# Row maxima over 1024 keys in one two-bank PSUM tile that a recurrence's first stage also uses

## The chip, the cores and the metric

One Trainium2 chip, one core. The metric is the device time of one execution in microseconds; the kernel before was run three times and its median is used. The profiled execution is a further one.

## The reference

Two layers of an encoder over 1024 tokens of width 1024. Each layer projects its input, runs four mixers side by side, and follows them with an output projection, a cross attention to 256 memory tokens and a mixture of experts, each with a layer norm. Two of the mixers are softmax attentions of four heads over all 1024 keys (GQA with head width 64, and MLA with 96); the other two are linear recurrences (RWKV-7 and HGRN2), in both directions. What matters here is the attention:

```
s = q . k * scale              (1024 queries x 1024 keys, per head)
p = exp(s - max over keys) / sum
o = p . v
```

## The kernel before

**The order.** Each layer's mixers are written as Python generators. `weave` advances two of them in proportion to given costs: `rwkv` (the RWKV-7 recurrence) and `beside`, which first runs the attention to its end and then HGRN2 and the preparation of the memory attention. That gives the order in which the program is written; the tile framework's scheduler then fixes one order per engine, in which instructions that are ready may pass others. On the chip each engine works through its own order and waits by semaphores.

**The attention** (lines 1398 to 1465) is cut into eight units per layer, each of two heads and 512 queries; four of GQA, then four of MLA. `row_max` computes, for a unit, the largest score of each query, with one pass of rounded operands: for each head j and each block t of 128 queries, two matmuls of 512 keys (line 1409), each into a PSUM tile of one bank, each followed by a VectorE maximum (line 1410) over its 512 columns. One more VectorE instruction joins the halves (line 1413); then, for each head, four small matmuls turn the maxima into a row (line 1417) and ScalarE copies that row, negated, into the 65th or 97th row of an operand (line 1418), so that the later score matmuls subtract the maximum. `attend` then takes the 1024 keys in eight steps of 128: score matmuls into tile `b` (line 1441), an exponential on ScalarE (line 1443), value matmuls into `o` (line 1429), and an addition on GpSimd that collects the denominators (line 1432). `attention` runs the `row_max` of one unit and the `attend` of the unit before it in lockstep, one step of each in turn, `attend` first; the row maxima of the first unit stand alone.

**The recurrence** runs up to four of its units at a time in lockstep, each in another stage. A unit's first stage uses PSUM tile `a0`: two gate matmuls (lines 961 and 966) that ScalarE reads through a tanh, and twice 32 small matmul records (line 1027) into two banks, each bank read by a masked VectorE product (line 1029). The later stages use `a1`.

**PSUM before**, eight banks of 512 floats per partition: `a0` two tiles of one bank, `a1` two, `b` two, `c` one (row maxima alone, and for the first unit `c`, `b`, `b` in turn), `o` one.

**Key buffers.** The rounded keys `kh0`, `kh1` and their remainders have one buffer per name. An MLA unit with new keys (the fifth and the seventh) therefore can't load them before the scores of the unit in front are done.

Of the kernel before, what the change touches and what calls it, by code (L numbers as in the profile page):

```python
# [13 lines left out]
S = 1024  # L14
# [168 lines left out]
F32R = mybir.dt.float32r  # L183
I32 = mybir.dt.int32
U32 = mybir.dt.uint32
AF = mybir.ActivationFunctionType
ALU = mybir.AluOpType
AX = mybir.AxisListType
PSUM = bass.MemoryType.PSUM
# [123 lines left out]
def ahead(gen):  # L313

    return chain([next(gen)], gen)
# [439 lines left out]
def lockstep(gens, group=0):  # L755

    gens = list(gens)
    while gens:
        n = 0
        for g in list(gens):  # L760
            try:
                c = next(g) or SMALL
            except StopIteration:
                gens.remove(g)
                continue
            n += c
            if not group:
                yield c
        if group:
            yield n  # L770
# [121 lines left out]
def rwkv_unit(k, e):  # L892

    nc, A, V, S, T, G = k.nc, k.A, k.V, k.S, k.T, k.G
    hp, d, hf, first, pl, lo, kn, kds, zr, zk, kept = (e[n] for n in (
        "hp", "d", "hf", "first", "pl", "lo", "kn", "kds", "zr", "zk", "kept"))
    hw, wa, seg, mask, blk4, lvl, id64 = (e[n] for n in ("hw", "wa", "seg", "mask", "blk4", "lvl", "id64"))
    w = 0

    def bank():  # L900
        return k.t(e["ps"], [128, 512], f"a{w}")

    def tl(shape, tag, bufs=1):
        return k.t(pl, shape, tag, bufs=bufs)
# [4 lines left out]
    q = lambda p: slice(64 * p, 64 * p + 64)  # L909

    def pairs(fn, cols, evac, byhead=False):


        if byhead:

            b = [bank() for _ in range(2)]
            for i in range(4):
                for h in range(2):
                    for p in range(2):
                        fn(b[h][:, cols * i:cols * i + cols], i, h, p)  # L920
            for h in range(2):
                evac(b[h][:, :4 * cols].rearrange("q (m c) -> q m c", c=cols), slice(h, 8, 2))
        elif cols == 128:
            for g in range(2):
                b = bank()
                for m in range(4):
                    i, h = divmod(4 * g + m, 2)
                    for p in range(2):
                        fn(b[:, cols * m:cols * m + cols], i, h, p)
                evac(b[:, :4 * cols].rearrange("q (m c) -> q m c", c=cols), slice(4 * g, 4 * g + 4))  # L930
        else:
            b = bank()
            for m in range(8):
                i, h = divmod(m, 2)
                for p in range(2):
                    fn(b[:, cols * m:cols * m + cols], i, h, p)
            evac(b.rearrange("q (m c) -> q m c", c=cols), slice(0, 8))
# [17 lines left out]
    j = 2 * d + hp  # L955
# [4 lines left out]
    b = bank()  # L960
# [4 lines left out]
    b = bank()  # L965
# [47 lines left out]
    if e["n"] == 3:  # L1013
# [3 lines left out]
        b = bank()  # L1017
# [8 lines left out]
    for x, dst in ((0, AB), (1, AK)):  # L1026
        pairs(lambda o, i, h, p: T.matmul(o[q(p)], BK[q(h), x, 2 * i + p], AR[q(h), :, 2 * i + p],
                                          start=True, stop=True),
# [7 lines left out]
    for pb in range(8):  # L1036
        b = pb % 4
# [12 lines left out]
    for n in range(1, 8):  # L1050
        s, r = (7 - n, slice(8 - n, 8)) if d == 0 else (n, slice(0, n))
# [6 lines left out]
    i, o = (lo_, hi_) if d == 0 else (hi_, lo_)  # L1058
# [19 lines left out]
    w = 1  # L1078
# [9 lines left out]
    def tok(src, dst):  # L1088
        b = bank().rearrange("q (i c) -> q i c", c=128)
        for i in range(4):  # L1090
# [5 lines left out]
                                         func=AF.Copy))  # L1096
    yield 1
    tok(BK[:, 0], lambda b: S.activation(out=AB.rearrange("q (i h) c -> q i h c", h=2)[:, :, :, 128:192],
                                         in_=b.rearrange("q i (h c) -> q i h c", h=2), func=AF.Copy))
# [16 lines left out]
    for v in range(2):  # L1116
# [9 lines left out]
        if v == 0:  # L1126
            pairs(lambda o, i, h, p: T.matmul(o[q(p)], XT[q(p), 0, 2 * i + h], ZZ[q(p), 2 * i + h],
                                              start=True, stop=True),
# [42 lines left out]
    for m, n in enumerate(order):  # L1171
# [9 lines left out]
        b = bank()[:, :64]  # L1181
# [28 lines left out]
def hgrn_load(k, Z, pool, hp, d):  # L1210
    x, R = (k.t(pool, [128, 1024], s) for s in ("hx", "h3"))
    k.nc.sync.dma_start(R, Z["h"][6 + 2 * d + hp])
    k.nc.sync.dma_start(x, Z["h"][2 + 2 * d + hp])
    return x, R
# [180 lines left out]
            yield  # L1395


def row_max(k, ps, heads, tags="c"):

    V, S, T = k.V, k.S, k.T
    nm = k.t(k.small, [128, 2, 4, 2], "nm")
    for j, ((q, kk), _, _, _) in enumerate(heads):
        for t in range(4):
            for c in range(2):
                s = tags[(8 * j + 2 * t + c) % len(tags)]
                b = k.t(ps, [128, 512], s, bufs=1 if s == "c" else None)
                T.matmul(b, q[:, 128 * t:128 * t + 128], kk[:, 512 * c:512 * c + 512], start=True, stop=True)  # L1409
                V.reduce_max(nm[:, j, t, c:c + 1], b, axis=AX.X)  # L1410
            yield
    mx = k.t(k.small, [128, 2, 4], "nmx", F32R)
    V.tensor_tensor(mx, nm[:, :, :, 0], nm[:, :, :, 1], ALU.max)
    for j, (_, _, row, _) in enumerate(heads):
        b = k.t(ps, [128, 512], "c", bufs=1)
        for t in range(4):
            T.matmul(b[0:1, 128 * t:128 * t + 128], mx[:, j, t:t + 1], k.ident_r, start=True, stop=True)
        S.activation(out=row, in_=b[0:1], func=AF.Copy, scale=-1.0)


def attend(k, pl, pe, ps, po, heads, scale, dst):
# [34 lines left out]
    yield  # L1456


def attention(k, units, pl, pe, ps, po):

    prev = None
    for heads, scale, dst in units:
        yield from lockstep([prev, row_max(k, ps, heads)], 1) if prev else row_max(k, ps, heads, "cbb")
        prev = attend(k, pl, pe, ps, po, heads, scale, dst)
    yield from prev

# [134 lines left out]
class Weights:  # L1601
# [62 lines left out]
    def next(self):  # L1664
        return self.ready.popleft()
# [590 lines left out]
def trunk(nc, tc, A, out, nl=2, dbg=None):  # L2256
    with ExitStack() as es:
        k = K(nc, tc, A, out, es, dbg)
        src = ahead(ln_in(k))
        k.setup()  # L2260
        trunk_consts(k, es)
        ppt = [k.cload(f"ppt{l}", A["pp"][l], [128, NPP]) for l in range(2)]
        for l in range(nl):
            def pp(n, i=None, t=ppt[l]):
                o, m = PP[n]
                return t[:, o:o + m] if i is None else t[:, o + i:o + i + 1]

            k.pp = pp
            mix_d = k.dt([8, 128, 1024], "mix")
            Z = in_proj(k, l, src)  # L2270
            with ExitStack() as es2:
                cp = k.pool(es2, "mixc")
                pa = k.pool(es2, "pa", 2)
                sa = k.pool(es2, "psa", 2, PSUM)
                wqk, vw = k.dt([4, 128, 4, 512], "wqk"), k.dt([4, 128, 4, 512], "vw")

                def beside():
                    pe = k.pool(es2, "pe", 1, side="right")
                    first = hgrn_load(k, Z, pe, 0, 0)
                    with ExitStack() as es3:  # L2280
                        pb = k.pool(es3, "pb", 1, side="right")
                        sb = k.pool(es3, "psb", 2, PSUM)
                        so = k.pool(es3, "pso", 1, PSUM)
                        units = chain(gqa(k, l, Z, mix_d, pb), mla(k, l, Z, mix_d, pb))
                        for _ in attention(k, units, pb, pe, sb, so):
                            yield ATT
                        raw = mem_load(k)
                    with ExitStack() as es3:
                        ph = k.pool(es3, "ph", 1, side="right")
                        sh = k.pool(es3, "psh", 2, PSUM)  # L2290
                        sm = k.pool(es3, "psm", 2, PSUM)
                        yield from weave([hgrn(k, Z, l, mix_d, cp, ph, sh, pe, first),
                                          mem_prep(k, l, raw, wqk, vw, ph, pe, sm)], SHARES)

                for _ in weave([rwkv(k, l, Z, mix_d, cp, pa, sa), beside()], (RW, SPLIT)):
                    pass
            with ExitStack() as es2:
                W = Weights(k, es2, weights(A, l, wqk, vw))
                n = nc.values_load(Z["wide"][0:1, 0:1], min_val=0, max_val=1, skip_runtime_bounds_check_because="a comparison")
                with tc.If(n > 0):  # L2300
                    with ExitStack() as es3:
                        cp = k.pool(es3, "mixc")
                        ph = k.pool(es3, "ph", 1)
                        sh = k.pool(es3, "psh", 2, PSUM)
                        for _ in hgrn(k, Z, l, mix_d, cp, ph, sh, general=True):
                            pass
                W.open()
                x2_d, lg, sl = mix_mem(k, l, mix_d, wqk, vw, W, k.pool(es2, "slots"))
                src = moe(k, l, x2_d, lg, sl, W)
                if "x2" in k.dbg:  # L2310
                    nc.sync.dma_start(k.dbg["x2"][l], x2_d)
                    nc.sync.dma_start(k.dbg["mix"][l], mix_d)
            src = ahead(src) if l == 0 else src
        for _ in src:
            pass
# [16 lines left out]
```

## Time and profile before

| | us |
|---|---|
| median of 3 runs | 3599.37 |
| lowest, highest | 3596.83, 3609.17 |
| profiled execution, own time | 3598.46 |
| its span in the profile | 3596.6 |

The span is what the profiler saw from first to last instruction. In this trace the attention of the first layer lies from about 357 to 765 us and that of the second from about 2128 to 2536 us. PE stands for TensorE's matmuls and PEld for its weight loads, DVE for VectorE, ACT for ScalarE, POOL for GpSimd.

### The profile page before, as it was taken

The numbers are of one execution on the slowest core, as the hardware profiler recorded it, in microseconds if no ns is written. First come the engines' busy times: TensorE is split into PE (matmuls) and PEld (weight loads), VectorE is DVE, ScalarE is ACT, GpSimd is POOL, SyncE is SP. The second block draws the span as 40 slices with busy tenths as digits, with TensorE's granted clock in tenths as the row PEclk, the third lists the DMA queues.
The fourth block names the chain that finished last, engine by engine and source line by source line (L and its number), as shares of the span: only waits on it lengthen the run. The fifth ranks groups of instructions, "written<-read, shape, count | busy, mean of one in ns | idle before, by whom it ended". The sixth has DMA issues, their size and how long they took to land. (4 is left out here: it accounts for less than half of the span.)

```text
span 3596.6 us, 57124 instructions
## 1 busy us (share of the span) xinstructions
PE 3179.0 (88%) x22814; PEld 2394.0 (67%) x22814; DVE 2489.7 (69%) x3966; ACT 1577.5 (44%) x2303; POOL 745.1 (21%) x496
## 2 busy tenths in 40 slices
PE   8999799988969997999599888989888699979995
PEld 7867345557857886777487564454677588867772
DVE  6546877668846466899764578767788364669996
ACT  3344333345432222788534353433454323138883
POOL 0000353421020003332210004533200200033323
PEclk9999799899989997999799988988899899979997
DMA  5223411125464132999542252111344741249994
GB/s 212 109 74 134 99 34 46 42 75 152 122 216 157 61 135 108 342 363 372 210 160 109 81 158 43 52 28 45 97 146 119 255 158 59 88 155 362 365 341 186
DMA packets 270217, 545.74 MB, mean 152 GB/s; under 512 B 90608, under 2 KB 170096, under 8 KB 236400
## 3 DMA queue, kind: packets, MB, share of 16 engines
q1 hardware_dynamic: 244496, 486.31, 39.5%
q0 software_dynamic: 24288, 53.52, 4.2%
q8 instruction: 184, 3.01, 0.3%
q10 hardware_dynamic: 1152, 2.10, 0.2%
q14 instruction: 97, 0.79, 0.1%
HBM read 444.29 MB, written 131.07 MB: 160 GB/s over the span
## 5 line engine op out<-in xcount | busy, mean ns | idle before, releaser
L1655 DVE TENSOR_TENSOR wl<-raw,wh 128x2048 fp32r<-128x2048 f32 x202 | 465.2, 2306 | 69.5 <-ACT wh L1654 66.6
L1654 ACT ACTIVATE wh<-raw 128x2048 fp32r<-128x2048 f32 x216 | 413.4, 1914 | 161.8 <-PE y L260 102.4
L1432 POOL TENSOR_TENSOR acc<-acc,pT 128x512 f32<-128x512 f32 x224 | 312.4, 1418 | 326.5 <-PE o L1429 197.0
L258 PE MATMUL bg<-wh,xh 128*128 128x512 f32 x768 | 310.3, 404 | 45.6 <-ACT xh L1696 45.6
L260 PE MATMUL bg<-wh,xl 128*128 128x512 f32 x768 | 307.9, 401 | 5.0 <-DVE xl L1697 4.9
L259 PE MATMUL bg<-wl,xh 128*128 128x512 f32 x768 | 308.2, 401 | 0.0
L1410 DVE TENSOR_REDUCE nm<-c 128x1 f32<-128x512 f32 x236 | 161.8, 685 | 109.8 <-PE c L1409 107.6
L1443 ACT ACTIVATE pT<-b 128x512 f32<-128x512 f32 x224 | 128.1, 595 | 211.2 <-PE b L1441 198.4
L719 PE MATMUL p<-xh,wh 128*128 128x512 f32 x640 | 208.1, 404 | 0.9 <-DVE r L569 0.9
L258 PE MATMUL h<-wh,xh 128*128 128x512 f32 x512 | 207.9, 406 | 0.2 <-ACT xh L309 0.2
L309 ACT ACTIVATE xh<-tp 128x512 fp32r<-128x512 f32 x224 | 122.9, 599 | 185.1 <-PE tp L307 175.7
L260 PE MATMUL h<-wh,xl 128*128 128x512 f32 x512 | 202.5, 395 | 0.0
L259 PE MATMUL h<-wl,xh 128*128 128x512 f32 x512 | 202.3, 395 | 0.0
L719 PE MATMUL p<-xl,wh 128*128 128x512 f32 x640 | 200.3, 392 | 0.0
L719 PE MATMUL p<-xh,wl 128*128 128x512 f32 x640 | 199.4, 391 | 0.0
L258 PEld LDWEIGHTS bg<-wh,xh 128*128 128x128 f32 x768 | 146.6, 191 | 79.1 <-ACT xh L1696 47.2
L1655 POOL TENSOR_TENSOR wl<-raw,wh 128x2048 fp32r<-128x2048 f32 x14 | 63.7, 4565 | 632.3 <-ACT wh L1654 616.9
L958 POOL DMA_DIRECT2D xs<-zlo x48 | 26.5, 556 | 779.3 <-DVE raw L512 660.6
L2078 POOL DMA_INDIRECT ya<-yo,slot x64 | 93.3, 1458 | 403.9 <-DMA ya<-yo,slot 178.1
L260 PEld LDWEIGHTS bg<-wh,xl 128*128 128x128 f32 x768 | 146.2, 190 | 40.3 <-DVE xl L1697 7.9
L259 PEld LDWEIGHTS bg<-wl,xh 128*128 128x128 f32 x768 | 146.6, 191 | 32.1
L310 DVE TENSOR_TENSOR xl<-tp,xh 128x512 fp32r<-128x512 f32 x224 | 146.1, 682 | 29.4 <-ACT xh L309 23.1
(518 smaller groups left out, 8023.5 us busy)
## 6 DMA issues: line engine op xcount, KB each, us to landing
raw<-in_moe_w_dram SPq DMA_DIRECT2D x192, 1024.0 KB
raw<-in_w_inb_dram SPq DMA_DIRECT2D x20, 1024.0 KB
x<-x SPq DMA_DIRECT2D x40, 512.0 KB
mz<-in_mem_wkv_dram SPq DMA_DIRECT2D x64, 256.0 KB
mz<-in_mem_wqt_dram SPq DMA_DIRECT2D x32, 256.0 KB
wqk<-rec SPq DMA_DIRECT2D x32, 256.0 KB
mz<-in_mem_wo_dram SPq DMA_DIRECT2D x32, 256.0 KB
vw<-rec SPq DMA_DIRECT2D x32, 256.0 KB
```

Of the source, the lines that this page charges most:

```text
L258: self.T.matmul(ps, ah, bh, start=start, stop=False)
L259: self.T.matmul(ps, ah, bl, start=False, stop=False)
L260: self.T.matmul(ps, al, bh, start=False, stop=stop)
L309: self.S.activation(out=h, in_=p, func=AF.Copy)
L310: self.V.tensor_tensor(xl[:, 4 * j:4 * j + 4], p, h.bitcast(F32), ALU.subtract)
L719: T.matmul(p[i], a, b[i][:, kk], start=(kk == 0 and a is h and b is xh), stop=(kk == 7 and a is lo))
L1410: V.reduce_max(nm[:, j, t, c:c + 1], b, axis=AX.X)
L1432: G.tensor_tensor(acc[j], acc[j], p[j], ALU.add)
L1443: S.activation(out=p[j], in_=b, func=AF.Exp, scale=scale)
L1654: k.S.activation(out=h, in_=raw, func=AF.Copy)
L1655: (k.G if pool else k.V).tensor_tensor(lo, raw, h.bitcast(F32), ALU.subtract)
L2078: G.indirect_dma_start(out=y_d, out_offset=bass.IndirectOffsetOnAxis(ap=ai, axis=0), in_=y, in_offset=None, bounds_check=2047, oob_is_err= ...
```

## The change

The row maxima lose their own bank `c`. They use tag `a0` of the recurrence's pool, which becomes one tile of two adjacent banks (1024 columns) with one buffer. Two matmuls fill its halves, and one VectorE instruction takes the maximum over all 1024 columns, so that the joining instruction goes. For the first unit of a layer, every second block uses two tiles `b` instead, with two maxima and a join. The rows of both heads are formed in one `a0` tile, eight small matmuls and then two copies. In the lockstep `row_max` now comes before `attend`. The bank that `c` had goes to `b`, which has three buffers. The first stage of the recurrence takes its single banks as the first half of such a tile, and its pairs of banks as both halves.

```diff
     def bank():
-        return k.t(e["ps"], [128, 512], f"a{w}")
+        return k.t(e["ps"], [128, 512], "a1") if w else k.t(e["ps"], [128, 1024], "a0", bufs=1)[:, :512]
+
+    def two():
+        if w:
+            return [bank() for _ in range(2)]
+        b = k.t(e["ps"], [128, 1024], "a0", bufs=1)
+        return b[:, :512], b[:, 512:]
...
-            b = [bank() for _ in range(2)]
+            b = two()
...
-def row_max(k, ps, heads, tags="c"):
+def row_max(k, ps, heads, pb=None):
     V, S, T = k.V, k.S, k.T
-    nm = k.t(k.small, [128, 2, 4, 2], "nm")
+    mx = k.t(k.small, [128, 2, 4], "nmx", F32R)
+    two = lambda: k.t(ps, [128, 1024], "a0", bufs=1)
     for j, ((q, kk), _, _, _) in enumerate(heads):
         for t in range(4):
-            for c in range(2):
-                s = tags[(8 * j + 2 * t + c) % len(tags)]
-                b = k.t(ps, [128, 512], s, bufs=1 if s == "c" else None)
-                T.matmul(b, q[:, 128 * t:128 * t + 128], kk[:, 512 * c:512 * c + 512], start=True, stop=True)
-                V.reduce_max(nm[:, j, t, c:c + 1], b, axis=AX.X)
+            lone = pb and t % 2
+            b = None if lone else two()
+            c = [k.t(pb, [128, 512], "b") for _ in range(2)] if lone else (b[:, 0:512], b[:, 512:1024])
+            for i in range(2):
+                T.matmul(c[i], q[:, 128 * t:128 * t + 128], kk[:, 512 * i:512 * i + 512], start=True, stop=True)
+            if lone:
+                nm = k.t(k.small, [128, 2], "nm")
+                for i in range(2):
+                    V.reduce_max(nm[:, i:i + 1], c[i], axis=AX.X)
+                V.tensor_tensor(mx[:, j, t:t + 1], nm[:, 0:1], nm[:, 1:2], ALU.max)
+            else:
+                V.reduce_max(mx[:, j, t:t + 1], b, axis=AX.X)
             yield
-    mx = k.t(k.small, [128, 2, 4], "nmx", F32R)
-    V.tensor_tensor(mx, nm[:, :, :, 0], nm[:, :, :, 1], ALU.max)
+    b = two()
     for j, (_, _, row, _) in enumerate(heads):
-        b = k.t(ps, [128, 512], "c", bufs=1)
         for t in range(4):
-            T.matmul(b[0:1, 128 * t:128 * t + 128], mx[:, j, t:t + 1], k.ident_r, start=True, stop=True)
-        S.activation(out=row, in_=b[0:1], func=AF.Copy, scale=-1.0)
+            n = 512 * j + 128 * t
+            T.matmul(b[0:1, n:n + 128], mx[:, j, t:t + 1], k.ident_r, start=True, stop=True)
+    for j, (_, _, row, _) in enumerate(heads):
+        S.activation(out=row, in_=b[0:1, 512 * j:512 * j + 512], func=AF.Copy, scale=-1.0)
...
-def attention(k, units, pl, pe, ps, po):
+def attention(k, units, pl, pe, ps, po, pm):
...
-        yield from lockstep([prev, row_max(k, ps, heads)], 1) if prev else row_max(k, ps, heads, "cbb")
+        yield from lockstep([row_max(k, pm, heads), prev], 1) if prev else row_max(k, pm, heads, ps)
...
-                        sb = k.pool(es3, "psb", 2, PSUM)
+                        sb = k.pool(es3, "psb", 3, PSUM)
...
-                        for _ in attention(k, units, pb, pe, sb, so):
+                        for _ in attention(k, units, pb, pe, sb, so, sa):
```

## Rows read from the trace of the kernel before

**Rows 1.** The page, busy time of each engine over the span.

```profile
PE 3179.0 (88%) x22814; PEld 2394.0 (67%) x22814; DVE 2489.7 (69%) x3966; ACT 1577.5 (44%) x2303; POOL 745.1 (21%) x496
```

**Rows 2.** Busy time by stretch: both layers' attention, and what follows it.

```profile
core 0: us, PE busy (x) PEld busy (x) DVE busy (x) ACT busy (x) POOL busy (x), PEclk, DMA share, GB/s
357.00:765.00 408.00, 364.67 (x2677) 195.06 (x2677) 298.31 (x494) 150.64 (x259) 175.15 (x138) 0.87 0.21 54
765.00:1045.00 280.00, 240.21 (x4114) 209.34 (x4110) 222.14 (x494) 136.86 (x242) 22.20 (x17) 0.96 0.46 139
2128.00:2536.00 408.00, 360.03 (x2674) 193.38 (x2675) 301.26 (x503) 150.63 (x259) 174.67 (x138) 0.87 0.21 55
2536.00:2826.00 290.00, 247.76 (x4116) 215.90 (x4112) 222.01 (x495) 136.15 (x242) 22.80 (x18) 0.93 0.44 132
```

**Rows 3.** Waits of PE from 357 to 765: total, times, longest (us).

```profile
PE c L1409 <- DVE nm L1410: 15.4, 23, 3.0
PE b L1441 <- ACT pT L1443: 4.0, 2, 3.6
...
PE b L1441 <- ACT ql L1418: 3.4, 1, 3.4
...
PE b L1441 <- DVE rec L1453: 3.1, 2, 2.3
...
PE c L1417 <- ACT ql L1418: 1.3, 2, 0.7
```

**Rows 4.** Waits of PE's weight loads in the same stretch.

```profile
PEld c L1409 <- DVE nm L1410: 38.6, 51, 3.9
```

**Rows 5.** Groups of instructions, first four from 357 to 765, last of the whole span.

```profile
L1410 DVE TENSOR_REDUCE nm<-c 128x1 f32<-128x512 f32 x118 | 80.9, 685 | 56.2 <-PE c L1409 55.1
...
L1027 PE MATMUL a<-AR,BK 64*64 64x128 f32 x352 | 25.7, 328 | 0.0
...
L1029 DVE TENSOR_TENSOR AB<-a,mask 128x512 f32<-128x512 f32 x12 | 8.0, 682 | 3.1 <-PE a L1027 3.1
...
L963 ACT ACTIVATE lw<-a,hw 128x512 f32<-128x512 f32 x6 | 4.1, 686 | 21.9 <-PE a L961 21.8
...
L1743 DVE TENSOR_REDUCE mx<-bg 128x4 f32<-128x1024 f32 x16 | 19.6, 1224 | 82.2 <-PE bg L260 82.2
```

**Rows 6.** Timeline of PE in a stretch without recurrence (start, us).

```profile
592.93 0.50 PE L1409 MATMUL c<-kh,qh 96*128 96x512 f32 x1
593.27 0.39 PE L1441 MATMUL b<-qh,kh 96*128 96x512 f32 x1
593.50 0.40 PE L1441 MATMUL b<-ql,kh 96*128 96x512 f32 x1
```

**Rows 7.** Timeline of PE while only row maxima and the recurrence run.

```profile
672.35 0.79 PE L1409 MATMUL c<-kh,qh 96*128 96x512 f32 x1 [0.78 <-DVE nm L1410]
...
687.15 0.79 PE L961 MATMUL a<-xs,wa 96*128 96x512 f32 x1
...
692.31 0.80 PE L1409 MATMUL c<-kh,qh 96*128 96x512 f32 x1 [0.37 <-DVE nm L1410]
...
693.89 0.80 PE L1409 MATMUL c<-kh,qh 96*128 96x512 f32 x1 [0.37 <-DVE nm L1410]
```

**Rows 8.** Timeline around the longest wait for `c`.

```profile
425.59 3.54 DVE L1495 TENSOR_TENSOR qh<-raw,qh 64x512 fp32r<-64x512 f32 x1
...
429.16 0.69 DVE L1410 TENSOR_REDUCE nm<-c 128x1 f32<-128x512 f32 x1
```

**Rows 9.** Busy time and granted clock in three stretches of 10 us (columns as in rows 2).

```profile
675.00:685.00 10.00, 9.25 (x60) 6.03 (x59) 6.54 (x13) 0.00 (x0) 0.00 (x0) 0.50 0.08 29
685.00:695.00 10.00, 8.53 (x38) 4.25 (x36) 8.01 (x16) 1.37 (x2) 1.61 (x3) 0.50 0.21 51
...
705.00:715.00 10.00, 10.00 (x30) 4.64 (x30) 9.77 (x18) 2.52 (x5) 9.92 (x8) 1.00 0.05 13
```

**Rows 10.** Timeline: last row of the sixth unit, first row maximum of the seventh.

```profile
624.57 0.58 ACT L1418 ACTIVATE qh<-c 1x512 fp32r<-1x512 f32 x1
...
662.29 0.49 PE L1409 MATMUL c<-kh,qh 96*128 96x512 f32 x1
```

## The prediction

> **What bounds the kernel now.** I read the page's engine table first: over the whole span PE is the busiest engine, but no engine is full [rows 1], so the stage that the change touches has to be read by itself. The windows do that: the two attention stages last 408 us each, 816 us of the span, and are alike; in each PE is busy 365 and 360 us, DVE about 300, ACT 151, POOL 175 [rows 2]. PE is thus the engine whose order sets the end of this stage, and 43 to 48 us per layer are what it stands idle. Everything behind an attention stage is woven behind it in the same engine orders, so a microsecond that PE saves here arrives earlier at the end; nothing of the stage behind it is done early.
>
> Next come the waits of that stretch. The largest wait of PE itself is for VectorE's maximum to free the bank `c`: 15.4 us in 23 pieces [rows 3]. The weight loads show 38.6 us in 51 more [rows 4], but most of those run while PE still streams an earlier matmul, so the reader should count only PE's own. The third view, the timeline, shows why the wait exists: the one bank `c` makes a strict chain of matmul, maximum, matmul. Where attention has nothing else to do, two neighbouring links lie 1.58 us apart [rows 7]; where VectorE is busy with something else, the chain stands (an operand subtraction of 3.54 us, and the maximum starts only behind it) [rows 8]. The fourth is the granted clock: 0.87 on average in the stage [rows 2], which at levels of 1 and 0.5 means 2 x 0.13 x 408 = 106 us at half speed. Such a stretch is 675 to 695, where the exponentials and additions rest and PE follows the chain; with full work on PE it is at 1.00 [rows 9].
>
> **The change part by part, per layer.**
>
> *VectorE's work.* 128 maxima at 0.685 [rows 5] are 87.7 us. After: 56 + 4 wide ones. The wide one is not in this kernel's attention, but another VectorE reduction reads 1024 columns of a two-bank PSUM tile in 1.224 us [rows 5]; I take that. 60 x 1.224 + 8 x 0.685 = 78.9, so 9 us less, the join added for the first unit and removed for the others being small. VectorE is busy 298 of 408 [rows 2], so these 9 us pay only through the waits below: 0 by themselves. If VectorE were the bound they would be worth the whole 9.
>
> *The wait for the bank.* Of the two waits of each step the first goes, since both matmuls write an empty tile; the other has a whole step, on average 408 / 80 = 5.1 us (eight steps alone for the first unit, then nine for each `attend`), for a chain that needs 0.73 (two matmuls, 0.23 apart in start as the scores in [rows 6], 0.50 for the last) + 1.22 + about 0.1 to hand over = 2.0. Bounds: 0 to the whole 15.4. VectorE's late starts [rows 8] stay, so I take two thirds, -10.
>
> The Trainium skill, page "Perfetto Trace Analysis", section "Optimizing Scalar/DVE Operations", says that where VectorE is not saturated but causes bubbles on another engine, breaking up instructions may let work finish sooner; this change does the reverse, and the first release after a tile's start comes after 1.22 instead of 0.685. By that rule the -10 would be 0, the gain 20 us smaller and the time 3581, still inside the forecast's own range. I side with the row of 1.58 per link, because the same PE wait is paid twice per tile today.
>
> *Fewer turns on PE.* A matmul behind one of another kind starts 0.34 after it, one of the same sort 0.23 [rows 6]: 0.11 for each of 64 matmuls that now follow their twin, -7. Bounds 0 and, at half clock, twice that.
>
> *Third buffer `b`.* It covers waits of scores for the exponential (4.0) and for the reciprocal that ends a unit (3.1) [rows 3]. A third tile lets one score pass go on but not more, since the exponential's own buffers stay two; -3, bounds 0 and -7.
>
> *Rows of the maxima and the new lockstep order.* The second head's small matmuls no longer wait for the first head's copy (1.3), and the next unit's scores wait less for the row (3.4, once) [rows 3]; `row_max` written ahead ends a unit's row about one step earlier. -3, bounds 0 and -5. The pair ahead of the scores delays them by 0.73; ACT and POOL, which wait behind, are busy under half of the stage [rows 2] and cover that; without the cover it is 64 x 0.73 = 47, but then PE would have no other work, which [rows 2] excludes. No DMA is issued in what is moved; the unit's loads stay where they are.
>
> *The shared tile.* This is the price. A wide tile is held 2.0 us, 64 x 2.0 = 128 of 408, 31%. Six recurrence units pass their first stage there [rows 5]: each has two gate tiles (0.50 + 0.69 = 1.2) and two pair tiles (25.7 / 11 = 2.3 for the matmuls, as 352 records are 11 tiles of 32, and 2 x 0.68 for the products: 3.7), 9.8 per unit, 59 us, 14%. A stage-one tile finds the buffer held in 31% and waits half of 2.0: 24 x 0.31 x 1.0 = 7. A row-max tile: 64 x 0.14 x 1.2 = 11. Having lost its second buffer, stage one waits for itself another 6 x (0.69 + 0.68) = 8. Sum 26, if nothing covers it. Today 15.4 of 15.4 + 38.6 us of waiting on `c` reach PE, 29% [rows 3, 4]; of 26 that is +8. Bounds +0 and +26.
>
> *The seventh unit.* Its first maximum comes 38 us after the last row of the sixth [rows 10], as its keys have one buffer. From 672.35 to 693.89 PE makes 11 links, and the gate matmul at 687.15 shows a recurrence unit in its first stage there [rows 7]. Two links of 1.58 become one of 2.5 at half clock (0.80 + 0.43 + 1.22 + 0.1): -0.66 for six tiles, -4. Against it four first-stage tiles, 9.8 us, of which today's slack of 11 x (1.96 - 1.58) = 4 has covered part, now share the chain. I take 0, bounds -4 and +6.
>
> *Clock.* If 10 of the 106 us at half speed come back, that is -5; bounds 0 and -20, since the long half-speed stretch around the seventh unit stays.
>
> *Sum:* -10 - 7 - 3 - 3 + 8 + 0 - 5 = -20 per layer; the second layer's stage is alike [rows 2], -40, and the first stage of the last recurrence units, which runs outside the window on one buffer, gives back 2 x 1: -38. The profiled execution took 3598.46 (span 3596.6 and what lies around it), 0.9 under the median of the three; from 3598.5 to 3560.5, and against the median 3561.
>
> **The rivals.**
>
> *Bigger gain.* The waits go whole and the clock gives 14 per layer: -15 - 7 - 7 - 5 + 8 - 14 = -40, so 3599 - 80 = 3519. For it: the long wait of [rows 8] sits at the head of a half-clock stretch. Against it: PE would then stand idle only about 15 us in the stage. 16%.
>
> *The waits change their name.* The maxima's waits stay and a bit over half of the 26 reaches PE: -7 - 3 - 3 + 15 = +2 per layer, 3603, within 0.3% of before (0.3%, 11 us, is about what three runs of this kernel can tell). The Trainium skill, same page, section "Matmuls", asks that independent groups of matmuls rotate through different PSUM banks so that the evacuation of one overlaps the next; here two users go onto one buffer, and by that rule alone all 26 would count and the forecast be 3561 + 2 x 18 = 3597, in this case's band. The rows bear it out only in that waits on the single `c` exist. 15%.
>
> *Slower: the first stage queues behind keys.* If the shared tile goes out in the order in which the program is written, a first-stage tile behind the seventh unit's first maxima waits until those keys are loaded: from 624.57 to 662.29, 38 us [rows 10]; the fifth unit has new keys too, for one of its heads, say half. The recurrence's later stages go on meanwhile, but its first stage is late by up to 57 us per layer. It decides once more than 20 us of that reach PE; at two thirds, 38 - 20 = +18 per layer, 3635. Against it: the scheduler may let ready instructions pass. Today's `c` has one user, so the trace can't say. 11%.
>
> *Slower by collisions.* All 26 reach PE, and the seventh unit costs +6: -10 - 7 + 32 = +15, 3630. 7%.
>
> **How the numbers follow.** My forecast (gain of 11 to 60 us) has 51%. With 16% for the bigger gain, faster by over 0.3% is 0.67; same 0.15; slower 0.18. The forecast's own range is 3538 to 3588. For 8 in 10 I reach to 3510, which takes in most of the bigger gain, and to 3615, which takes in no change and the milder half of the slower cases.
>
> **What the profile after would show.** The name `c` is gone from the attention; 120 reductions of 128x1024 at about 1.22 us stand under line 1410's successor. PE's wait for them falls from 15.4 to about 5 per layer; if it stays at 15, the step on the bank is wrong. The two attention stages last about 388 instead of 408. Waits of the gate and pair matmuls of the recurrence (lines 961, 966, 1027) for the maxima appear, 5 to 10 us on PE; over 20 and the shared tile is the story. If the stretch between the sixth and seventh unit is longer than now, the third rival is at work. A mean clock in the stage below 0.87 would also prove me wrong.

## The result, and the profile after

The changed kernel takes 3578.85 us (median of 9 runs, 3563.33 to 3590.65); the kernel before, on the same chips in the same session, 3596.83 (9 runs, 3587.56 to 3609.17). The ratio is 0.995, 95% interval 0.9929 to 0.9971: 18 us faster, between 10 and 26. I had forecast 3561, a gain of 38 us: right in sign, inside the range of 3538 to 3588, and about twice too large. The profiled execution of after (3563.33) is the shortest of the nine, so whoever holds the two profiles against each other sees 35 us. A second profile of the changed kernel, at 3582.68, shows where that flatters: the two attention stages are 25 us shorter than before in the first and 19 in the second, and the rest of the span took 2794.5 us in the first, 2808.1 in the second and 2804.5 before: 14 us apart in two profiles of one kernel.

From here on I therefore measure the **attention stretch**: from the start of the first row-max matmul to the start of the last exponential, in each layer. Before: 396.5 and 395.6 us. After, in three profiles in which its attention is the same (this one, after_again and dve_more below): 382.4, 384.6; 387.1, 385.7; 382.0, 384.1. The mean is 384.3, the spread 2.8 either way, the gain 11.7 per layer.

Busy time of the two attention stages of after, the answer to [rows 2] (in front the stretch and its length; then PE, PEld, DVE, ACT, POOL, granted clock, DMA share, GB/s):

```profile
core 0: us, PE busy (x) PEld busy (x) DVE busy (x) ACT busy (x) POOL busy (x), PEclk, DMA share, GB/s
357.00:751.00 394.00, 344.96 (x2641) 180.33 (x2641) 278.76 (x415) 149.35 (x259) 171.19 (x138) 0.88 0.22 55
2115.00:2513.00 398.00, 347.62 (x2636) 182.96 (x2636) 281.46 (x423) 148.86 (x259) 171.38 (x138) 0.87 0.22 56
```

408 us became 394 and 398, where I expected 388. PE stands idle 49 and 50 us of it, not less than before (43 and 48): what went is busy time of PE (365 to 345) and of VectorE (298 to 279). The clock is 0.88 and 0.87.

Waits of PE in the first of these stages, the answer to [rows 3] (waited for: total, times, longest, us):

```profile
PE b L1455 <- ACT pT L1457: 6.2, 2, 5.1
PE a L1417 <- DVE nmx L1424: 6.0, 7, 1.3
PE a L1430 <- DVE nmx L1424: 5.3, 4, 1.6
...
PE a L1417 <- DVE AB L1035: 3.4, 1, 3.4
PE a L1417 <- ACT P L974: 2.7, 4, 0.8
```

And of its weight loads, the answer to [rows 4]:

```profile
PEld a L1417 <- DVE nmx L1424: 11.2, 9, 2.0
```

The wait for the bank fell from 15.4 to 6.0 as forecast, but other waits stand beside it: the small matmuls of the row (line 1430) wait 5.3 for the last maximum, where it was 0.9 before, and under two new names row maxima wait 3.4 and 2.7 for the recurrence's products (line 1035) and gate (line 974), which now hold the same tile. The wide maximum costs what I took from the 1024-column reduction of [rows 5]; here is its group on the page of after, over the whole span:

```profile
L1424 DVE TENSOR_REDUCE nmx<-a 128x1 fp32r<-128x1024 f32 x120 | 146.3, 1220 | 117.0 <-PE a L1417 116.6
```

The chain of the seventh unit has the link that the prediction worked out. Timeline of PE in after, counterpart of [rows 7]:

```profile
660.81 1.22 PE L1417 MATMUL a<-kh,qh 96*128 96x512 f32 x2 [0.97 <-DVE nmx L1424]
663.34 1.22 PE L1417 MATMUL a<-kh,qh 96*128 96x512 f32 x2 [1.32 <-DVE nmx L1424]
665.88 1.22 PE L1417 MATMUL a<-kh,qh 96*128 96x512 f32 x2 [1.32 <-DVE nmx L1424]
```

One link per 1024 keys is 2.53 us; predicted was 2.5, against 2 x 1.58 before.

### The profile page after: what moved, and what is told of

It reads as the page before. It is cut to its first block, busy times and chain, and to the rows that moved or that the text cites. A ratio compares the mean times of both kernels' runs of the same rounds, so it can differ in the third digit from the quotient of the medians.

```text
span 3561.5 us, 57014 instructions
## 1 busy us (share of the span) xinstructions
PE 3158.1 (89%) x22814; PEld 2370.4 (67%) x22814; DVE 2457.0 (69%) x3838; ACT 1576.9 (44%) x2303; POOL 732.8 (21%) x496
## 5 line engine op out<-in xcount | busy, mean ns | idle before, releaser
L1424 DVE TENSOR_REDUCE nmx<-a 128x1 fp32r<-128x1024 f32 x120 | 146.3, 1220 | 117.0 <-PE a L1417 116.6
L1443 PE MATMUL o<-pT,v 128*64 128x512 f32 x448 | 174.6, 642 | 0.3
```

The lines of the kernel that those rows point to most:

```text
L1424: V.reduce_max(mx[:, j, t:t + 1], b, axis=AX.X)
L1443: T.matmul(o[64 * j:64 * j + 64], v[:, s], p[j], start=(s == 0), stop=(s == 7))
```

## The experiments

The question after the result: the bank wait fell as forecast, so what ate half of the gain? My theory was the shared tile, under-priced at +8 per layer; the rivals were that VectorE's time, order of issue or the third `b` pay otherwise than I said. The table has every run; the edits and readings follow. Stretches are layers 0 and 1; the ratio is to the kernel before.

| run | stretches, us | median, us | ratio, 95% interval |
|---|---|---|---|
| before | 396.5, 395.6 | 3596.8 | 1 |
| changed kernel | 382.4, 384.6 | 3578.85 | 0.995 [0.9929, 0.9971] |
| after_again | 387.1, 385.7 | 3582.68 | 0.9953 [0.9933, 0.9973] |
| order_only | 396.3, 397.4 | 3597.57 | 0.9999 [0.9985, 1.0014] |
| old_order | 382.2, 381.4 | 3574.79 | 0.9937 [0.9918, 0.9957] |
| two_b | 382.2, 375.3 | 3570.6 | 0.991 [0.9882, 0.9938] |
| two_maxima | 394.3, 395.0 | 3600.29 | 1.0005 [0.9983, 1.0028] |
| late_join | 392.6, 388.3 | 3588.84 | 0.9976 [0.9963, 0.9989] |
| dve_more | 382.0, 384.1 | 3574.34 | 0.9931 [0.9918, 0.9944] |
| dve_after | 392.3, 394.9 | 3597.12 | 1.0008 [0.9993, 1.0023] |
| stage_on_a1 | 368.1, 370.9 | 3552.34 | 0.9876 [0.9859, 0.9892] |
| banks_in_turn | 372.4, 375.3 | 3559.15 | 0.9896 [0.9881, 0.991] |
| own_in_turn | 374.0, 368.8 | 3562.97 | 0.9899 [0.9879, 0.9919] |
| own_three | 380.8, 378.0 | 3570.98 | 0.9924 [0.9905, 0.9943] |

### Again, unchanged (after_again)

> The changed kernel once more, beside the kernels below. The first profile of it was 35 us shorter than that of before, while the medians of nine runs lie 18 us apart; its attention stretches (first row-max matmul to last exponential) took 382.5 and 384.7 us instead of 396.5 and 395.7. If the gain sits in those stretches, a second profile shows the same lengths to about 1 us, with PE's wait for the wide maximum at 6.0 us per layer, whatever the whole run takes, and the rest of the difference lies in stages that the change doesn't touch. If the first profile was a lucky one in the attention itself, the stretches come out near 390.

No edit. It repeats the result and gives the spread above.

### The order alone (order_only), and the change without it (old_order)

```diff
-        yield from lockstep([prev, row_max(k, ps, heads)], 1) if prev else row_max(k, ps, heads, "cbb")
+        yield from lockstep([row_max(k, ps, heads), prev], 1) if prev else row_max(k, ps, heads, "cbb")
```

> The kernel before with one edit: row_max stands ahead of attend in the lockstep; bank c, its 512-column maxima and two tiles b stay. Theory 1, the paired matmuls give the gain: this alone gives nothing, stretches of 396 us within 2, time within 0.3% of before (3586 to 3608). Theory 2, the order gives it (rows are ready a step earlier): stretches near 385, PE's wait for c unchanged at about 15 us, time about 18 us under before.

In the kernel before, the maxima put ahead give nothing (0.9999), and yet the wait that I had set out to remove shrinks. Waits of PE from 357 to 765 in this run:

```profile
PE c L1409 <- DVE nm L1410: 9.5, 17, 1.3
PE c L1409 <- ACT ql L1418: 4.0, 2, 3.5
PE b L1441 <- DVE rec L1453: 3.6, 2, 2.8
```

The 15.4 of [rows 3] became 9.5 and the time stayed. The wait did not only change its name, for all of PE's idle time fell, from 43.3 us before [rows 2] to 37.4; but its busy time rose by as much, from 364.67 to 370.64, for as many matmul records (2674 and 2677) and at a granted clock of 0.90 instead of 0.87:

```profile
357.00:765.00 408.00, 370.64 (x2674) 193.06 (x2672) 299.14 (x498) 150.40 (x259) 172.59 (x138) 0.90 0.21 52
```

Why they stand for more time is open. A share of idle time is thus no gain in hand. The opposite edit takes the new order out of the changed kernel:

```diff
-        yield from lockstep([row_max(k, pm, heads), prev], 1) if prev else row_max(k, pm, heads, ps)
+        yield from lockstep([prev, row_max(k, pm, heads)], 1) if prev else row_max(k, pm, heads, ps)
```

> The changed kernel with the old order of issue: in each step the scores first, then the row maxima. Wide tile, sharing and three b tiles as in the changed kernel. Order put ahead gave nothing in the kernel before (ratio 0.9999). If it gives nothing here either: 3575 to 3585, stretches 381 to 388. If the order is what lets the maximum run under the scores on the single wide tile (each block's maximum of 1.22 us has the score products of its step behind it): stretches 390 to 396, median 3592 to 3605, PE's wait for row maxima above 12 us per layer.

381.8 on the mean: the order gives nothing here either.

### Two tiles `b` instead of three (two_b)

```diff
-                        sb = k.pool(es3, "psb", 3, PSUM)
+                        sb = k.pool(es3, "psb", 2, PSUM)
```

> The changed kernel with two tiles b instead of three (one bank stays unused). The prediction gave the third 3 us per layer; but PE's waits in front of the scores for the exponential and the reciprocal hardly changed (7.1 us before, 7.5 after). If the third tile gives nothing, the stretches stay at 383 to 385 us; if it hides what the new order costs, they grow by 5 us or more each, and the time by 10 or more.

One bank lies unused, and the time is not longer (0.991 against 0.995, the intervals overlap). The third `b` pays nothing.

### VectorE's time (dve_more, dve_after)

```diff
                 V.reduce_max(mx[:, j, t:t + 1], b, axis=AX.X)
+            V.reduce_max(k.t(k.small, [128, 1], "idle"), k.ident, axis=AX.X)
```

> The changed kernel with one more VectorE instruction per block of queries, a maximum over 128 columns of a constant that nobody reads, about 0.28 us, so 18 us per layer; nothing is left out of the output. Theory 4: stretches of 395, the gain gone, as with the two maxima and their joins. If VectorE's time counts for nothing by itself, as the prediction had it, 385 and no change of time against the changed kernel.

A miss of the design: the added reductions read only a constant, and all of them were put at 8 to 89 us of the span, long before attention. The attention is that of the changed kernel, and serves as its third profile. The second try hangs the extra work on the maximum just made, and nothing reads it:

```diff
                 V.reduce_max(mx[:, j, t:t + 1], b, axis=AX.X)
+                V.reduce_max(k.t(k.small, [128, 1], "idle"), mx[:, j, t:t + 1].bitcast(F32).to_broadcast([128, 256]), axis=AX.X)
```

> The changed kernel with one more VectorE reduction per block, over 256 copies of the block's maximum, right behind the wide maximum; nothing reads it, and it holds no PSUM tile, but it can't start before the maximum. Some 0.35 us each by half of a 512-column maximum (0.685 us), 60 to 64 per layer: 21 to 23 us more of VectorE in each attention stretch. The prediction's step (VectorE's saved time is worth nothing by itself): median 3575 to 3585, stretches 381 to 388. The rival (0.56 us of stretch per us of VectorE, as the run with the late join can be read): stretches 394 to 398, median 3600 to 3606.

The groups of VectorE in its first attention stretch (367.0 to 759.3):

```profile
L1424 DVE TENSOR_REDUCE nmx<-a 128x1 fp32r<-128x1024 f32 x60 | 73.1, 1219 | 47.1 <-PE a L1417 46.5
L1425 DVE TENSOR_REDUCE idle<-nmx 128x1 f32<-128x256 f32 x60 | 24.4, 407 | 0.3
```

24.4 us more of VectorE, which hold no PSUM tile, make the stretch 393.6 - 384.3 = 9.3 longer (and the median 3597.1 - 3578.9 = 18.2, or 9.1 per layer): 0.38 us for each us, or 0.27 to 0.50 with the spread of 2.8. "0 by themselves" was wrong, and the rival's 0.56 was too high. The added reductions hold no tile, but they stand in the queue in which the recurrence's products wait, so part of their price may be the shared tile's; no run measures it without the sharing.

### The maximum's width on the shared tile (two_maxima, late_join)

In both, the tile stays wide and shared, but two maxima of 512 columns read it; two_maxima joins them per block, late_join once per unit, as before the change.

```diff
-            if lone:
+            if True:
                 nm = k.t(k.small, [128, 2], "nm")
                 for i in range(2):
                     V.reduce_max(nm[:, i:i + 1], c[i], axis=AX.X)
                 V.tensor_tensor(mx[:, j, t:t + 1], nm[:, 0:1], nm[:, 1:2], ALU.max)
-            else:
-                V.reduce_max(mx[:, j, t:t + 1], b, axis=AX.X)
```

> The changed kernel, but the shared two-bank tile is read by two maxima of 512 columns and a join instead of one of 1024. The two matmuls still follow each other, and the tile is still freed once. Theory 1, the pair on PE gives the gain: it stays, stretches of 383 to 386 us, VectorE 9 us busier per layer, time within 0.3% of the changed kernel. Theory 3, the wider instruction gives it: stretches near 394, and about 15 us of the 18 are gone.

```diff
+    nm = k.t(k.small, [128, 2, 4, 2], "nm")
...
+            for i in range(2):
+                V.reduce_max(nm[:, j, t, i:i + 1], c[i], axis=AX.X)
             yield
+    V.tensor_tensor(mx, nm[:, :, :, 0], nm[:, :, :, 1], ALU.max)
```

> The changed kernel with two maxima of 512 per tile, as in the earlier run, but one join per unit instead of one per block: VectorE does what it did in the kernel before, while the matmuls are paired and share the tile. That earlier run (64 joins, about 18 us of VectorE more per layer than the changed kernel) lost the whole gain: stretches of 394.6 us on average, against 385.0 of the changed kernel and 396.0 of before. Theory 4, VectorE's time counts: a line through these points (pairing -6, 0.56 us per us of VectorE) gives 390 here and a time near 3588. Theory 3, only the single long instruction counts (it frees the tile at once): still 394 to 396, 3597. Theory 1, pairing alone: 385, 3580.

Their stretches are 394.7 and 390.5 on the mean, 10.4 and 6.2 longer than those of the changed kernel. For late_join the added work is 60 x (2 x 0.682 - 1.219) = 8.7 us of VectorE while the tile is held, so 0.71 us for each if the joins, under 2 us more, are left aside. But two_maxima has these 8.7 and 60 more joins of 0.310 behind them, 27 us, and costs 0.38 for each, as dve_after does. Its groups of VectorE, from 365 to 761:

```profile
L1421 DVE TENSOR_REDUCE nm<-a 128x1 f32<-128x512 f32 x120 | 77.2, 682 | 55.4 <-PE a L1417 55.3
L1422 DVE TENSOR_TENSOR nmx<-nm 128x1 fp32r<-128x1 f32 x64 | 19.9, 310 | 0.3
```

With a spread of 2.8 us the two rates don't differ: that VectorE's time costs more while it holds the tile is not shown. The Trainium skill's rule that the prediction weighed (page "Perfetto Trace Analysis", section "Optimizing Scalar/DVE Operations", breaking up instructions) isn't borne out on this tile, which both halves must leave before it is free: the broken-up maximum is the slower one (390.5 against 384.3). Where each half has a bank that is freed by itself, it is the faster one (banks_in_turn below, 373.9).

### The recurrence's first stage on banks of its own (stage_on_a1)

```diff
-        return k.t(e["ps"], [128, 512], "a1") if w else k.t(e["ps"], [128, 1024], "a0", bufs=1)[:, :512]
+        return k.t(e["ps"], [128, 512], "a1")
...
-        if w:
-            return [bank() for _ in range(2)]
-        b = k.t(e["ps"], [128, 1024], "a0", bufs=1)
-        return b[:, :512], b[:, 512:]
+        return [bank() for _ in range(2)]
```

The first stage now takes the two one-bank tiles of the recurrence's later stages; the wide tile is the row maxima's alone.

> The changed kernel, but the recurrence's first stage takes the one-bank tiles a1 of the later stages instead of the shared tile, so the row maxima have their two banks alone. PE's waits at the shared tile for the other user (gate tanh, masked product, row copies) are 9 us per layer in the profile of the changed kernel; the prediction had 8. If that is the price of sharing, these waits go and the stretches shorten by up to 9 us, to 376, unless a1 takes the same price: then PE waits for a1 appear and it stays at 385.

369.5 on the mean: 14.8 us per layer shorter than the changed kernel, 26.5 shorter than before, and by its median the fastest kernel of this study (3552.34, 0.9876). The sharing costs about 15 per layer (13 by the medians), not 8, set against a first stage that must share `a1` instead. Where it is paid shows when the stretch is cut where the second attention unit ends (at its reciprocal). First before, then after, then this run, columns as above:

```profile
365.60:481.40 115.80, 95.55 (x675) 49.65 (x676) 94.97 (x160) 45.62 (x80) 46.61 (x39) 0.83 0.33 78
481.40:763.10 281.70, 262.18 (x1952) 140.14 (x1952) 196.21 (x319) 99.63 (x171) 125.69 (x96) 0.88 0.15 41
```

```profile
365.00:485.80 120.80, 98.69 (x706) 50.01 (x710) 91.61 (x142) 47.46 (x82) 44.76 (x39) 0.79 0.31 75
485.80:748.50 262.70, 239.25 (x1886) 125.51 (x1878) 181.39 (x259) 96.65 (x169) 122.76 (x96) 0.92 0.17 44
```

```profile
364.70:468.40 103.70, 86.93 (x678) 47.35 (x678) 96.16 (x141) 46.23 (x82) 49.23 (x39) 0.87 0.36 84
468.40:733.80 265.40, 239.26 (x1908) 131.48 (x1906) 191.10 (x261) 97.05 (x170) 123.78 (x96) 0.91 0.17 44
```

After gains 19 us behind the cut and loses 5 ahead of it; without the sharing the part behind is the same within the spread (265), and the part ahead is 17 shorter. The second layer has the same picture: 17 shorter ahead of the cut and 4 longer behind it. So the whole price falls in the first third, where two recurrence units pass their first stage and a third its gates. The timeline shows how. After, the second recurrence unit, whose pair operands are complete at 402.93 (line 1011); PE and VectorE, the shared tile's users and what VectorE does between them:

```profile
402.25 0.68 DVE L1011 TENSOR_TENSOR BK<-P,AK 128x512 f32<-128x512 f32 x1
...
407.44 1.10 PE L1033 MATMUL a<-AR,BK 64*64 64x128 f32 x32
...
410.34 1.64 DVE L1069 TENSOR_TENSOR LP<-LA,LX 64x512 f32<-64x512 f32 x1
...
412.62 0.67 DVE L1035 TENSOR_TENSOR AB<-a,mask 128x512 f32<-128x512 f32 x1
413.22 2.05 DVE L1073 TENSOR_TENSOR LP<-LX 64x512 f32<-64x512 f32 x1
415.19 0.68 DVE L1035 TENSOR_TENSOR AB<-a,mask 128x512 f32<-128x512 f32 x1
...
416.01 1.19 PE L1417 MATMUL a<-kh,qh 128*128 128x512 f32 x2 [3.44 <-DVE AB L1035]
...
417.24 1.23 DVE L1424 TENSOR_REDUCE nmx<-a 128x1 fp32r<-128x1024 f32 x1 [0.37 <-PE a L1417]
...
422.94 1.98 PE L1033 MATMUL a<-AR,BK 64*64 64x128 f32 x32
...
424.99 1.29 DVE L1035 TENSOR_TENSOR AK<-a,mask 128x512 f32<-128x512 f32 x2 [6.52 <-PE a L1033]
```

The same unit with the first stage on banks of its own:

```profile
402.54 1.10 PE L1030 MATMUL a<-AR,BK 64*64 64x128 f32 x32 [0.85 <-DVE BK L1002]
...
405.83 0.68 DVE L1032 TENSOR_TENSOR AB<-a,mask 128x512 f32<-128x512 f32 x1
...
407.36 1.72 PE L1030 MATMUL a<-AR,BK 64*64 64x128 f32 x32
...
412.33 0.67 DVE L1032 TENSOR_TENSOR AK<-a,mask 128x512 f32<-128x512 f32 x1
```

In after, the first pair tile holds the shared buffer from 407.44 to 415.87, 8.4 us, because its two products stand in VectorE's queue behind the solve of the unit before (lines 1069, 1073). The next row maximum waits for it: 3.44 us in which PE is idle. Then that maximum takes the tile until 418.47, and the second pair tile is multiplied only at 422.94, behind the scores and values queued ahead of it. The first stage ends at 426.3; with banks of its own the pairs run from 402.54 to 413.0.

This is no typical hold. Of the ten pair tiles of the stretch it is the longest, and their mean is 3.9 us. But it is there each time: 8.4 us at the same place in the second layer and in both layers of after_again. In these four stretches the second unit's first stage ends 61 to 66 us into the stretch, and the third unit's first gate comes at 72 to 76; in the two of this run the stage ends at 48 and 53, and the gate comes at 52 and 55.

The sums of the waits don't tell it: this fastest kernel shows more waiting of PE for the maximum than after does (357 to 751):

```profile
PE a L1414 <- DVE nmx L1421: 11.4, 12, 1.9
```

### Narrow maxima in two banks taken in turn, shared (banks_in_turn) and own (own_in_turn)

Both: 512-column maxima in one-bank tiles of `a0` (two of them), joined once per unit, order and three `b` as in the changed kernel. They differ in one line, whether the recurrence's first stage uses `a0` too.

```diff
-    two = lambda: k.t(ps, [128, 1024], "a0", bufs=1)
+    nm = k.t(k.small, [128, 2, 4, 2], "nm")
...
+                c = k.t(pb, [128, 512], "b") if lone else k.t(ps, [128, 512], "a0")
+                T.matmul(c, q[:, 128 * t:128 * t + 128], kk[:, 512 * i:512 * i + 512], start=True, stop=True)
+                V.reduce_max(nm[:, j, t, i:i + 1], c, axis=AX.X)
```

The line that differs, in `bank()`, first shared, then own:

```diff
+        return k.t(e["ps"], [128, 512], "a1") if w else k.t(e["ps"], [128, 512], "a0")
```

```diff
+        return k.t(e["ps"], [128, 512], "a1")
```

> Row maxima and first stage share the two banks of a0 as two one-bank tiles handed out in turn, each with its own 512-column maximum, one join per unit; order, three tiles b and the rest as in the changed kernel. The evacuation of one bank can run beside the matmul into the other. If rotation is what counts, PE's wait for the maxima falls below the 6.0 us of the wide tile and the stretches reach 385 or less with 9 us more of VectorE; by theory 4 they come to 390 to 396.

> The row maxima keep the old width: two 512-column maxima per block, in two one-bank tiles taken in turn that the recurrence's first stage does not use (it has the two a1 banks alone), joined once per unit. Order and three b tiles as in the changed kernel. To be set beside the run with the first stage on a1 and the wide tile (attention stretches 368.1 and 370.9 us, median 3552) and beside the run with banks in turn that are shared (372.4 and 375.3, 3559). Theory A (one wide tile is a serial loop: multiply, hand over, maximum, hand over; two banks in turn let the next product run under the maximum before): 6 to 12 us shorter per layer than the wide private tile, stretches 358 to 364, median 3530 to 3545, no wait of PE for a row maximum above 3 us. Theory B (VectorE's time counts, 9 us more of it per layer at 0.5 us each): 4 to 6 us longer per layer, stretches 373 to 376, median 3560 to 3565. Theory C (what counts is that the first stage does not wait for row maxima; width and turns are both hidden): stretches 367 to 372, median 3548 to 3556.

With stage_on_a1 and the changed kernel these make a square, mean stretch in us: wide and shared 384.3, wide and own 369.5, narrow in turn and shared 373.9, narrow in turn and own 371.4. Three corners agree within the spread; one is 10 to 15 longer. By the medians, in the same order 3578.85, 3552.34, 3559.15 and 3562.97, it is 16 to 27 us longer over both layers. Neither the sharing nor the one buffer costs much by itself: the two together do. With two banks in turn and shared, 66 of the 240 matmuls of row maxima into `a0` start while a maximum still reads the other bank, and 11 while a pair tile of the recurrence is held; in the changed kernel no such matmul does either. The two banks hide even the longer narrow maxima (128 x 0.682 = 87 us against 60 x 1.219 + 8 x 0.68 = 79). The theory that a private pair of banks in turn beats the private wide tile by 6 to 12 us fell. Its rival of 4 to 6 the other way stays open: the stretches say 1.9, but own_in_turn was profiled in its shortest execution, 3555.16, and its median lies 10.6 us above that of stage_on_a1 over both layers, with intervals that overlap.

The agreement is one of sums. Cut as above, narrow and shared is 6 us longer than narrow and own ahead of the cut and 3 shorter behind it, on the mean of both layers: some of the sharing's price is left in the first third, and is made up later.

Beside these numbers stands the rule that the prediction weighed, the Trainium skill, page "Perfetto Trace Analysis", section "Matmuls": independent groups should rotate through different PSUM banks. The runs agree with it for a buffer of two users, at 10 us per layer (384.3 against 373.9), and show no difference clear of the spread where the buffer has one user (369.5 against 371.4).

### Three banks for the maxima, two `b` (own_three)

```diff
-                c = k.t(pb, [128, 512], "b") if lone else k.t(ps, [128, 512], "a0")
+                c = k.t(pb, [128, 512], "b") if lone else k.t(ps, [128, 512], "c", bufs=3)
...
-                        sb = k.pool(es3, "psb", 3, PSUM)
+                        sb = k.pool(es3, "psb", 2, PSUM)
```

> As the kernel with its own two banks in turn, but three banks for the row maxima, the third taken from the scores (two b tiles). If the bank wait of the row maxima is still what ends last (theory A carried on), 3 to 6 us shorter per layer than with two banks, median 3520 to 3540, and the waits of PE for a score bank stay under 10 us per layer, as in the run with two b tiles. If the two banks already hide it, the time is within 5 us of the kernel with two. If the third b tile was needed once the row maxima run ahead freely, the waits of PE for ACT's exponentials grow by 5 us or more per layer and the time with them.

379.4 on the mean, 8 longer than with two banks, and 4 per layer by the medians, where the intervals overlap. PE's waits of `b` for exponentials (ACT) are 8.5 us here and 7.6 in own_in_turn, too little to explain it. A third bank gains nothing; whether and why it loses stays open.

## Why the prediction was right in sign and twice too large

**Removing the bank wait and the turns** (-10 and -7): right as a sum with the clock's -5, and not shown one by one. With the sharing taken away the attention gains 26.5 per layer (stage_on_a1), and the forecast's terms without the shared tile make -10 - 7 - 3 - 3 - 5 = -28. That these come so close is in part luck: two of the terms were nothing and one was left out (below), and what remains, -10 - 7 - 5 and VectorE's 3.4, is -25. The row of the wait can't bear out the -10: it fell by 9.4 in the changed kernel, but only by 4.0 in stage_on_a1, which gains the most, and by 5.9 in order_only, which gains nothing. The gain doesn't hang on the wide maximum: two banks in turn give much of it too, so what counts is that the maxima have two banks instead of one. Whether moving the first stage onto `a1` gains something by itself was not run; banks_in_turn doesn't move it and has 22 of the 26.5.

**The shared tile** (+8, bounds 0 to 26) is the step that failed, by its size: 14.8 per layer, measured by taking the sharing away. Over two layers that is 13.6 us of the 18 by which the forecast was off. The holds in its working were about right: in after a wide tile is held 2.4 us on the mean (worked out: 2.0) and a pair tile 3.9 (3.7). What failed is the way from there to the time, the 29% that came from the waits of one chain: 14.8 of the 26 is 57%, and the price is no average over the stretch. It falls in the first third, where one pair tile is held for 8.4 us since its products queue on VectorE, and where the recurrence's first stage comes late, which is no wait with the tile's name. [rows 8] showed such a queue, 3.54 us, for the row maxima, and I did not carry it over to the other user. That the stage is late in the same way in both layers is shown; how much of the 14.8 is due to that one hold is not.

**VectorE's 9 us** (0 by themselves): wrong by a little. At 0.38 per us, as dve_after measures it on the changed kernel, they are worth 3.4 per layer.

**Third `b`** (-3) and **rows and order** (-3): nothing, by two_b, order_only and old_order; the rows in one tile were not run by themselves. PE's wait of `b` for the exponentials, which the third was to cover, is 6.2 us and not 4.0 as before, and the small matmuls did not lose their wait, they have 5.3 us of one. That these two terms fell away and VectorE's came in (+6 - 3.4) brings the sum to -20 + 6.8 + 2.6 = -11 per layer; measured is -11.7, with the -10, -7 and -5 in it untested one by one.

**The seventh unit** (0): right. By the reciprocals that end the units, the seventh and eighth together took 106.0 us before and 104.5 after; the link of 2.53 was worked out right, and the sixth recurrence unit's first stage moved from the seventh attention unit into the eighth.

**Clock** (-5): at 1 and 0.5 for the two levels, 2 x 0.12 x 394 = 95 and 2 x 0.13 x 398 = 103 us at half speed, against 106 before, 3 to 11 back. I did not test it apart.

**The rivals.** The time fell between the forecast and the waits that change their name (3603). order_only has that rival's outcome, a smaller wait and no gain, but not its mechanism: PE's idle time fell, and its busy time rose. The first stage did not queue behind keys: the sixth recurrence unit's gate came 357 us into the stretch and not 322 as before, but without the sharing it comes at 343 (stage_on_a1) or 349 (own_in_turn) too, and the two attention units' time was unchanged. The bigger gain was not had, but 26.5 per layer of its 40 is there once the tile is not shared.

What the prediction named as signs: 120 wide reductions at 1.22 came, the wait fell to 6, the stages shrank to 394 and 398 and not to 388, and between the last row of the sixth unit and the first maximum of the seventh lie 35 us and not 38. One sign came the other way round: of the 5 to 10 us in which gate and pair matmuls wait for the maxima only 0.4 came, while the maxima's matmuls wait 8 us for gates, products and row copies. That is within what I had called harmless, and the price was 15 all the same.

## What to carry to other kernels

Before two producers are put on one single-buffered PSUM tile, look for the place where the instruction that empties it stands in a queue, and ask whose lateness follows: bare durations gave the mean hold here (3.7 against 3.9 us) and missed the one of 8.4. A pair of one-bank tiles in turn cost 2 to 5 us per layer more than the private wide tile, not clear of the noise, where the shared wide tile cost 15. A wait that disappears from one row of the waits is no gain until the stretch is shorter: order_only took 6 us out of the row and nothing out of the time, and the fastest kernel had the larger row. A probe of an engine's time must depend on the work beside which it is to stand, or it can end up elsewhere, as dve_more did.

## What the runs showed of the hardware

A VectorE maximum took 0.276 us over 128 columns and 0.407 over 256 (dve_more and dve_after, read from SBUF), 0.682 over 512 and 1.220 over 1024 (two_maxima and after, from PSUM): in both pairs 1.02 to 1.05 ns per column and some 0.14 us whatever the length. That fixed part, 0.14 per instruction and so about 9 us per layer, is all that the wide maximum saves. And VectorE's time, on an engine that is busy 273 of 383.5 us of the stretch, was worth 0.38 us each in the changed kernel (dve_after), though the added instructions held no PSUM tile.

PE's busy time is no fixed sum of work: with as many matmuls and a granted clock of 0.90 instead of 0.87, order_only had 6 us more of it and 6 us less idle time than before, in the same 408 us.
